# Making the first two tiles of W_out beside the last T stage, with their rows and turned halves in freed token spaces

## The chip, the cores and the metric

The kernel runs on one core of a Trainium2 chip. The metric is the device time of one execution in microseconds. A profiled execution gives a trace of every instruction on the core's engines: PE (TensorE matmul), PEld (its weight load), DVE (VectorE), ACT (ScalarE), POOL (GpSimd), and SP (SyncE), whose queue issues all the DMAs here. SP takes its DMAs strictly one after the other, and each waits for its own data and buffers.

## The reference

A two-layer encoder trunk on 2048 tokens of width 1024. Per layer, eight heads of banded softmax attention with a relative bias and four heads of chunkwise retention share one input projection, and their gated outputs go through `W_out` onto the residual:

```python
def hybrid_layer(x, norm_gain, w_in, w_out, rel_bias, cos, sin):
    hn = rms_norm(x, norm_gain)
    proj = hn @ w_in.astype(hn.dtype)
    aq, ak, av, ag, rq, rk, rv, rg = jnp.split(proj, cuts, axis=-1)
    ya = chunked_rel_attention(aq, ak, av, rel_bias)      # own chunk of 64 and 8 before it
    yr = chunkwise_retention(rq, rk, rv, cos, sin)        # with an RMS norm per head
    y = jnp.concatenate([ya * silu(ag), yr * silu(rg)], axis=-1)
    return x + y @ w_out

def reference(x, positions, norm_gain, w_in, w_out, rel_bias, final_gain):
    cos, sin = rotary_tables(positions, RET_HEAD_DIM)
    for layer in range(2):
        x = hybrid_layer(x, norm_gain[layer], w_in[layer], w_out[layer], rel_bias[layer], cos, sin)
    return rms_norm(x, final_gain)
```

## The kernel before

**Numbers.** Every large product is made in three float16 terms: each operand is split into an upper half and a rest ("hi" and "lo", "h" and "l"), and high·high, high·low and low·high are summed in PSUM. So each tile that a matmul uses exists as two float16 tiles.

**Stages.** A layer goes through four slices of heads (`s` = 0 to 3: two attention heads and one retention head each), and in each slice through four groups of 512 tokens (`n` = 0 to 3). For each `(s, n)` there are two dense stages: **T** (`dense_T`, L731), which makes q, k and the rotated retention q and k with features on partitions, and **V** (`dense_V`, L752), which makes the values and gates with tokens on partitions. Each stage has 96 matmuls in twelve parts ("thirds"). Attention and retention of the group before (`attention`, eight units of one 128-token tile and one head, three steps each) are interleaved: one step per third, so that its 24 steps lie beside one T and one V stage. After the last group of the last slice, **wout** (L1105) runs 16 token tiles × 6 rounds of 8 matmuls, and attention of the last group lies beside its first 24 rounds.

**Order.** The orders on PE, ACT, DVE and POOL are those in which the program records the instructions. SP's order is chosen by the scheduler, which moves loads to earlier places. Smaller work comes as generators that are pushed on a list (`push(gen, steps)`) and taken from its front (`pull`). `run` spreads the steps that the list still owes over the thirds that are left:

```python
for _ in gen:
    tick()
    if att[0] is not None and next(att[0], att) is att:
    ...
    if bg:
        pull(min(-(-todo // max(left, 1)), todo))
    left -= 1
```

`later(k, fn)` puts a function off by `k` thirds, and `tick` runs those that are due.

**An attention unit** (`qk`). PE makes S (L800, L801) in a PSUM tile of which there is one. DVE adds the bias and takes the maximum (L804, L806) into an `sc` buffer, ACT takes the exponential (L807) and its upper half into a `pq` buffer (L809), POOL makes the rest (L810). One third later a DMA transpose turns `pq` into `pT` (L812), and PE multiplies it with the values (L820 to L822) two units later. The tags `sc`, `pq` and `pT` have two buffers each.

**The output tiles.** Slices write their parts of a token tile's `y` to DRAM (`y_d`). For `wout` each tile comes back (`y_load`, L944), gets a power-of-two scale from its sum of squares (`y_squares` on ACT, L958; `y_scale`, five small DVE operations from L961), is split into two float16 rows (`rows_hi` on ACT, L227; `rows_lo` on DVE, L233), and both are turned by a DMA transpose (`y_turn`, L236 and L237). The rows come from `row_pair`, one buffer of tag `sc` and one of `pq`, that is from attention's two-buffer rings. The turned halves go into the tags `tabc` and `tabs` (even tiles) or `qq` and `swp` (odd tiles), which T stages use for the rotary tables and for q and k on their way (L670 is the multiplication with the tables). The residual's x is loaded into the space of a token group (`x_load`, L953).

**Token spaces.** `hT_of(l, n)` gives two float16 tiles (hTh, hTl) of 8 × 512 columns for the normalised tokens of group n. There are four such pairs. The spaces of one layer are handed to the next in the order of first request. After slice 3 has passed group n, its space is no longer read.

**Around the change.** `wout_first` makes the rows of tiles 0 and 1 and turns tile 0. It is pushed after the T stage of `(3, 3)`, with ten steps. `prep_O(l, 1)`, which converts the second half of `W_out` (L330 on ACT, L333 on DVE), is pushed right behind it with nine, so that both lie beside the V stage of `(3, 3)`. Tile 1 is turned in wout's second round (by program order). `rests` (L766 to L770) are the DVE operations that release a V stage's PSUM tile, one third after its matmuls.

Of the kernel before, what the change touches and what calls it, by code (L numbers as in the profile page):

```python
# [10 lines left out]
F32 = mybir.dt.float32  # L11
# [7 lines left out]
P = 128  # L19
# [8 lines left out]
def hybrid_trunk(ctx: ExitStack, tc: tile.TileContext, x, pos, gain, gcol, w_in, w_out, rel, fgain,  # L28
                 invf, dmask, dcol, out):
    nc = tc.nc  # L30
    SEQ, D = x.shape
    DEPTH = w_in.shape[0]
    KT = D // P
    NT = SEQ // P
    NS = SEQ // 512
    NSW = 4
# [119 lines left out]
    def gain_load(l):  # L156
        g = gains[l]
        g.b = cp.tile([P, D], F32, tag="gb", name=f"gb{l}")
        sp.dma_start(g.b, gain[l:l + 1, :].to_broadcast([P, D]))
# [40 lines left out]
    hT = {}  # L200
# [14 lines left out]
    def hT_of(l, n):  # L215
        if (l, n) not in hT:
            hT[l, n] = (hp.tile([P, KT, 512], F16, tag="hTh", name=f"hTh{l}_{n}"),
                        hp.tile([P, KT, 512], F16, tag="hTl", name=f"hTl{l}_{n}"))
        return hT[l, n]

    def row_pair(nm):
        return (b2.tile([P, 1280], F16, tag="sc", name=f"rh{nm}")[:, 0:D],
                b2.tile([P, 1280], F16, tag="pq", name=f"rl{nm}")[:, 0:D])

    def rows_hi(rows, xt, s_=None):

        act.activation(rows[0], xt, AF.Copy, scale=1.0 if s_ is None else s_[:, 0:1])  # L227

    def rows_lo(rows, xt, s_=None):
        if s_ is None:  # L230
            dve.tensor_tensor(rows[1], xt, rows[0], op=ALU.subtract)
        else:
            dve.scalar_tensor_tensor(out=rows[1], in0=xt, scalar=s_[:, 0:1], in1=rows[0], op0=ALU.mult, op1=ALU.subtract)  # L233

    def transpose_rows(rows, dh, dl):
        sp.dma_start_transpose(out=dh, in_=rows[0])  # L236
        sp.dma_start_transpose(out=dl, in_=rows[1])  # L237
# [350 lines left out]
    def flow(k=0):  # L588

        if len(pipe) > k:  # L590
            pipe.pop(0)()
# [344 lines left out]
    def y_load(l, t):  # L936
        u = St()
        u.nm = f"y{l}_{t}"
        u.t = t
        if t < 8:  # L940
            u.y = w4.tile([P, D], F32, tag="w4", name=f"yy{u.nm}")
        else:
            u.y = b2.tile([P, D], F32, tag="q", name=f"yy{u.nm}")
        sp.dma_start(u.y, y_d[t])  # L944
        return u

    def x_load(l, u):
        if l + 1 == DEPTH or u.t < 12:
            f = (hT[l, 0] if l + 1 == DEPTH else hT_of(l + 1, NS - 1))[u.t // 2 % 2].rearrange("p k c -> p (k c)").bitcast(F32)
            u.x = f[:, u.t % 2 * D:(u.t % 2 + 1) * D]  # L950
        else:
            u.x = w4.tile([P, D], F32, tag="w4", name=f"xx{u.nm}")
        sp.dma_start(u.x, x[u.t * P:(u.t + 1) * P, :] if l == 0 else x_d[u.t])  # L953

    def y_squares(u):
        u.m = b2.tile([P, 1], F32, tag="ym", name=f"ym{u.nm}")
        u.rows = row_pair(u.nm)
        act.activation(u.rows[0], u.y, AF.Square, accum_out=u.m)  # L958

    def y_scale(u, go):  # L960
        dve.tensor_scalar(u.m, u.m, 2.0 ** -100, None, op0=ALU.max)  # L961
        u.sy, iy = norm_scale(u.m, u.nm)
        u.sc = b2.tile([P, 1], F32, tag="osc", name=f"osc{u.nm}", bufs=4)
        dve.tensor_tensor(u.sc, iy, go.oi, op=ALU.mult)

    def y_turn(u):
        if u.t + 1 == NT:
            u.h, u.lo = (b2.tile([P, 10, P], F16, tag="pT", name=f"y{c}{u.nm}")[:, 0:KT, :] for c in "hl")
        else:
            u.h = b1.tile([P, KT, P], F16, tag=("tabc", "qq")[u.t % 2], name=f"yh{u.nm}")  # L970
            u.lo = b1.tile([P, KT, P], F16, tag=("tabs", "swp")[u.t % 2], name=f"yl{u.nm}")
        transpose_rows(u.rows, u.h, u.lo)
# [78 lines left out]
        sp.dma_start(out[t * P:(t + 1) * P, :], xt)  # L1051

    def wout_first(l, go, us):
        us.append(y_load(l, 0))
        x_load(l, us[0])
        us.append(y_load(l, 1))
        u, v = us
        for fns in ((), (lambda: y_squares(u),), (lambda: y_scale(u, go),), (lambda: rows_hi(u.rows, u.y, u.sy),),
                    (lambda: rows_lo(u.rows, u.y, u.sy), lambda: y_squares(v)), (lambda: y_turn(u), lambda: y_scale(v, go)),
                    (lambda: rows_hi(v.rows, v.y, v.sy),), (lambda: rows_lo(v.rows, v.y, v.sy),)):  # L1060
            yield
            for fn in fns:
                fn()
        yield

    def wout(l, go, gc, us, wT=None):

        end = l + 1 == DEPTH
        halves = [(t, c) for t in range(NT) for c in range(2)]
        if not end:  # L1070
            halves[-3], halves[-2] = halves[-2], halves[-3]
        events = {}
        for r in range(6 * NT):
            T, i = divmod(r, 6)
            t, c = halves[r // 3]
            u = us[t]
            if ring["att_done"] and i % 3 == 1:
                flow()
            for fn in events.pop(r, ()):
                fn()  # L1080
            hurry = T + 3 == NT and not end
            if i == 0 and 0 < T < NT - 1 and (end or T + 2 < NT):
                rows_lo(us[T + 1].rows, us[T + 1].y, us[T + 1].sy)
            if (i == 1 and T + 1 < NT and (end or T + 2 < NT)) or (i == 5 and hurry):
                y_turn(us[T + 1 if i == 1 else T + 2])
            if i == 0 and T + 2 < NT:
                us.append(y_load(l, T + 2))
            if i == 1 and T + 1 < NT:
                x_load(l, us[T + 1])
            if T + 2 < NT:  # L1090
                v = us[T + 2]
                if i == 3 - hurry:
                    y_squares(v)
                if i == 4 - hurry:
                    y_scale(v, go)
                if i == 5 - hurry:
                    rows_hi(v.rows, v.y, v.sy)
                    if hurry:
                        rows_lo(v.rows, v.y, v.sy)
            if i % 3 == 0:  # L1100
                ps = psD.tile([P, 512], F32, tag="dense", name=f"dO{l}_{t}_{c}")
            for m in range(8 * (i % 3), 8 * (i % 3) + 8):
                kt, w = divmod(m, 3)
                h_, w_ = ((u.h, gc[c].vh), (u.h, gc[c].vl), (u.lo, gc[c].vh))[w]
                pe.matmul(ps, h_[:, kt, :], w_[:, kt, :], start=(m == 0), stop=(m == 23))  # L1105
            if i % 3 == 2:
                xs = u.x[:, c * 512:(c + 1) * 512]
                keep(dve.scalar_tensor_tensor(out=xs, in0=ps, scalar=u.sc[:, 0:1], in1=xs, op0=ALU.mult, op1=ALU.add))
                if end and t + 1 == NT:
                    final_half(t, u.x, c)  # L1110
                if c == 1:
                    at = lambda k, fn, r=r: events.setdefault(r + k, []).append(fn)
                    if not end:
                        sp.dma_start(x_d[t], u.x)
                        rows = [w_[:, 2 + t % 2].rearrange("p k c -> p (k c)") for w_ in (wT.g.h, wT.g.l)]
                        residual(l + 1, t, u.x, at, rows if t < 4 else None, 4 < t < 12 and t % 4 > 0)
                    elif t + 1 < NT:
                        final(t, u.x, at)
            yield
        rest = [fn for r in sorted(events) for fn in events[r]]  # L1120
        push((fn() for fn in rest), len(rest))
        yield
# [5 lines left out]
    def push(gen, steps):  # L1128
        bg.append([gen, steps])
# [132 lines left out]
            self.s = [s_.bitcast(F32)[:, k:k + 1] for k in range(w)]  # L1262
            self.i = [i_.bitcast(F32)[:, k:k + 1] for k in range(w)]

    far = [hT_of(0, n) for n in (0, NS - 1, NS - 2)][1:]
    late = [h_.rearrange("p k c -> p (k c)").bitcast(F32)[:, i * D:(i + 1) * D] for f in far for h_ in f for i in range(2)]
    vst = [late[4 + j].rearrange("p (k c) -> p k c", c=P) for j in range(4)]
    x_in(0)
# [102 lines left out]
    for l in range(DEPTH):  # L1371
        gO = [Grp(), Grp()]
        go = Grp()
        for s in range(NSW):
            g = grp(l, s)
            for n in range(NS):
# [26 lines left out]
                        push(prep_O(l, 0, gO[0], go), 9)  # L1403
                if n == NS - 1 and s == 1 and l + 1 < DEPTH:
                    gain_load(l + 1)
                if not first:
                    run(dT, att, 10 if n == 0 else 14 if (l, s, n) == (0, 0, NS - 1) else 22 if (l, s) == (0, 0) else 24)
                if n == NS - 1 and s == NSW - 1:
                    us = []
                    push(wout_first(l, go, us), 10)  # L1410
                if n == 2 and s == 2:
                    push(prep_Omax(l, go), 13)
                if n == NS - 1:
# [19 lines left out]
        if l + 1 == DEPTH:  # L1433
            ring["fg"] = b3.tile([P, D], F32, tag="wh", name="fg")
            sp.dma_start(ring["fg"], fgain.to_broadcast([P, D]))
        wT = Sections(l + 1, 0, grp(l + 1, 0), True) if l + 1 < DEPTH else None
        wo = wout(l, go, gO, us, wT)

        def rounds_of(k):
# [76 lines left out]
```

## Time and profile before

| what | us |
|---|---|
| median of three timed runs | 2095.43 (2093.11 to 2095.86) |
| the profiled execution | 2094.75 |
| its span in the trace | 2092.8 |
| PE busy in the span | 2004.4 (96%) |
| DVE, ACT, POOL busy | 1343.8, 1141.3, 432.9 |
| mean granted TensorE clock | 0.991 |

In the trace, layer 0's T stage of `(3, 3)` runs from 833.4 to 859.4 us, its V stage to 893.2, and its wout stage to 1086.9. In layer 1 the same three run from 1846.3 to 1872.3, to 1906.0, and to 2085.5. A matmul's row has its start and its own length, which is longer than the distance to the next one since matmuls are pipelined. The pace is the distance between starts.

### The profile page before, as it was taken

What the parts mean: (1) busy time and instruction counts of PE and PEld (TensorE: products, weight loads), DVE (VectorE), ACT (ScalarE), POOL (GpSimd) and SP (SyncE); (2) the same over time, 40 slices, a digit from 0 to 9 for tenths busy, and PEclk for the clock granted to TensorE, in tenths of its full rate; (3) what the DMA queues carried; (4) which work ended last, traced back from release to release, by engine and by line L of the source; (5) the groups of instructions that cost most, each with busy time, mean ns of one, the idle gap of its engine ahead of it and who ended that gap; (6) DMA issues with size and microseconds to landing.
All of it is one profiled execution on the core that took longest, in us unless ns stands there. A gap on an engine that the chain in (4) does not pass through costs nothing.

```text
span 2092.8 us, 39599 instructions
## 1 busy us (share of the span) xinstructions
PE 2004.4 (96%) x14014; PEld 1049.4 (50%) x14014; DVE 1343.8 (64%) x4031; ACT 1141.3 (55%) x2522; POOL 432.9 (21%) x509
## 2 busy tenths in 40 slices
PE   6888999999999999998999999999999999998998
PEld 4344455555555555444444555555555555554443
DVE  7676666666656666576654666666666667656643
ACT  7455665556565654455444546554655565455432
POOL 1022222222122212121000222222222222222100
PEclk9999999999999999999999999999999999999999
DMA  8767674557476764599965556655655776558874
GB/s 247 171 127 162 136 166 114 115 112 159 110 169 133 161 166 99 113 211 260 219 185 113 120 102 142 130 121 106 155 123 118 178 156 162 117 100 183 212 199 123
DMA packets 645702, 313.65 MB, mean 150 GB/s; under 512 B 459232, under 2 KB 602080, under 8 KB 645504
## 3 DMA queue, kind: packets, MB, share of 16 engines
q1 hardware_dynamic: 645504, 311.12, 66.4%
q8 instruction: 110, 1.80, 0.4%
q14 instruction: 88, 0.72, 0.1%
HBM read 123.26 MB, written 41.98 MB: 79 GB/s over the span
## 4 chain that ended last, share of the span: by engine, by line
PE 55%; DMA 7%; DVE 5%; ACT 3%; issue 1%; SPq 1%; POOL 0%; POOLq 0%; DVEq 0%; ACTq 0%
PE dT L731 18%; PE dV L752 15%; PE dO L1105 12%; DMA pT<-pq 2%; PE r L860 2%; PE S L801 2%; PE S L800 2%; PE o L820 1%; PE o L821 1%; PE o L822 1%; DVE sc L804 1%; DMA swp<-rot 1%; DMA yhy<-rhy 1%; ACT sc L807 1%; ACT pq L809 1%
## 5 line engine op out<-in xcount | busy, mean ns | idle before, releaser
L810 POOL TENSOR_TENSOR pq<-sc,pq 128x640 f16<-128x640 f32 (+4 forms) x256 | 323.8, 1265 | 1175.9 <-issue 590.7
L807 ACT ACTIVATE sc<-sc,mq,cT 128x640 f32<-128x640 f32 (+4 forms) x256 | 218.5, 853 | 558.1 <-DVE mq L806 413.7
L752 PE MATMUL dV<-whV,hTh 128*128 128x512 f16 x1024 | 354.5, 382 | 13.0 <-DVE gt L770 12.8
L731 PE MATMUL dT<-hTh,whT 128*128 128x512 f16 x1008 | 349.4, 382 | 14.7 <-DMA hTh<-hTl 9.6
L752 PE MATMUL dV<-wlV,hTh 128*128 128x512 f16 x1024 | 354.1, 381 | 0.0
L752 PE MATMUL dV<-whV,hTl 128*128 128x512 f16 x1024 | 354.0, 381 | 0.0
L731 PE MATMUL dT<-hTl,whT 128*128 128x512 f16 x1008 | 346.6, 379 | 0.0
L731 PE MATMUL dT<-hTh,wlT 128*128 128x512 f16 x1008 | 346.6, 379 | 0.0
L752 PEld LDWEIGHTS <-hTh 128*128 128x128 f16 x2048 | 197.3, 98 | 227.7 <-DVE gt L770 16.4
L731 PEld LDWEIGHTS <-whT 128*128 128x128 f16 x2016 | 192.9, 98 | 221.6 <-issue 24.1
L804 DVE CUSTOM_DVE_ANT_0 sc<-S,bias 128x640 f32<-128x640 f32 (+4 forms) x256 | 188.4, 736 | 78.8 <-PE S L801 61.1
L1105 PE MATMUL dO<-whO,yly 128*128 128x512 f16 x512 | 194.1, 379 | 2.4 <-DMA yly<-rly 2.4
L1105 PE MATMUL dO<-whO,yhy 128*128 128x512 f16 x512 | 194.0, 379 | 1.2 <-DVE gt L770 0.6
L1105 PE MATMUL dO<-wlO,yhy 128*128 128x512 f16 x512 | 194.0, 379 | 0.0
L809 ACT ACTIVATE pq<-sc 128x640 f16<-128x640 f32 (+4 forms) x256 | 171.5, 670 | 10.9 <-DMA pT<-pq 3.0
L1105 PEld LDWEIGHTS <-yhy 128*128 128x128 f16 x1024 | 99.6, 98 | 115.1 <-issue 0.8
L752 PEld LDWEIGHTS <-hTl 128*128 128x128 f16 x1024 | 99.7, 98 | 105.0 <-issue 2.8
L800 PE MATMUL S<-k,q 128*128 128x128 f16 (+3 forms) x592 | 143.1, 268 | 7.9 <-DVE mq L804 7.9
L731 PEld LDWEIGHTS <-wlT 128*128 128x128 f16 x1008 | 97.2, 98 | 101.8 <-issue 1.1
L820 PE MATMUL o<-v,pT 128*128 128x65 f16 x1120 | 129.6, 193 | 10.2 <-DMA pT<-pq 9.7
L801 PE MATMUL S<-k,q 128*128 128x128 f16 (+3 forms) x592 | 130.5, 268 | 0.0
L820 PEld LDWEIGHTS <-pT 128*128 128x128 f16 x1120 | 105.3, 97 | 49.2 <-DMA pT<-pq 21.3
(350 smaller groups left out, 3352.7 us busy)
## 6 DMA issues: line engine op xcount, KB each, us to landing
q<-qq SPq DMA_DIRECT2D x128, 128.0 KB, 2.7
yyy<-y_d SPq DMA_DIRECT2D x32, 512.0 KB, 4.6
stT<-in_w_in_dram SPq DMA_DIRECT2D x27, 512.0 KB, 4.8
stV<-in_w_in_dram SPq DMA_DIRECT2D x26, 512.0 KB, 4.5
k<-kk SPq DMA_DIRECT2D x128, 64.0 KB, 2.0
swp<-rot SPq DMA_DIRECT2D x64, 128.0 KB, 2.5
tabc<-tab SPq DMA_DIRECT2D x32, 256.0 KB, 2.7
tabs<-tab SPq DMA_DIRECT2D x32, 256.0 KB, 2.9
```

Source lines behind the costliest of these rows:

```text
L731: pe.matmul(ps, w_[:, j, kt, :], h_[:, kt, :], start=(m == 0), stop=(m == 23))
L752: pe.matmul(ps, h_[:, kt, a * P:(a + 1) * P], w_[:, kt, :], start=(m == 0), stop=(m == 23))
L800: pe.matmul(o, st.q[:, hx, 0, cs], k_, start=True, stop=False)
L801: pe.matmul(o, st.q[:, hx, 1, cs], k_, start=False, stop=True)
L804: dve.tensor_tensor_reduce(out=v, in0=S[:, 0:w], in1=g.bias[hx][:, 640 - w:640], scale=1.0, scalar=-3.0e38, op0=ALU.add, op1=ALU.max, accu ...
L807: act.activation(v, v, AF.Exp, bias=m[:, 0:1], scale=g.c[:, 0:1])
L809: act.activation(pq[:, 0:w], v, AF.Copy)
L810: pool.tensor_tensor(pq[:, w:2 * w], v, pq[:, 0:w], op=ALU.subtract)
L820: pe.matmul(o[:, 0:65], u.p[:, b, :], v_[:, 0:65], start=(b == 0), stop=False)
L821: pe.matmul(o[:, 0:64], u.p[:, b, :], v_[:, 65:129], start=False, stop=False)
L860: pe.matmul(out_, w_, m_, start=(i == 0), stop=(i + 1 == len(pairs)))
L1105: pe.matmul(ps, h_[:, kt, :], w_[:, kt, :], start=(m == 0), stop=(m == 23))
```

## The change

- `wout_first` is pushed before the T stage of `(3, 3)`, with 14 steps, and now makes both tiles wholly, with their transposes. By the changed program's order its first twelve steps (tile 0 whole, tile 1 up to its squares) lie beside T, and the rest of tile 1 beside the start of V.
- `areas(l)` names three freed token spaces: those that the next layer's groups 3, 1 and 2 will use (in the last layer the spaces of its own groups 0, 1 and 2). The first holds x, as before.
- The rows of tiles 0 to 5 (in the last layer of all tiles) lie in quarters of the second and third space instead of the `sc` and `pq` rings. The turned halves of tiles 0 and 1 lie in the second space instead of `tabc`, `tabs`, `qq` and `swp`.
- `wout` no longer turns tile 1.
- The first request for the layer-0 spaces is in the order 0, 1, 2, 3 (it was 0, 3, 2, 1).
- On SP, as the scheduler orders it, tile 0's transposes stand before the attention transpose of the third unit of `(3, 2)`, and tile 1's before that of the sixth. In layer 0 the x loads of tiles 2 and 3 stand at the start of wout, where they stood in slice 3's first groups.

PE's instructions keep their number and order.

```diff
+    def areas(l):
+
+        if l + 1 == DEPTH:
+            return [hT[l, i] for i in range(3)]
+        return [hT_of(l + 1, i) for i in (NS - 1, 1, 2)]
+
+    def quarter(area, i):
+        return area[i // 4].rearrange("p k c -> p (k c)")[:, i % 4 * D:(i % 4 + 1) * D]
+
     def x_load(l, u):
         if l + 1 == DEPTH or u.t < 12:
-            f = (hT[l, 0] if l + 1 == DEPTH else hT_of(l + 1, NS - 1))[u.t // 2 % 2].rearrange("p k c -> p (k c)").bitcast(F32)
+            f = areas(l)[0][u.t // 2 % 2].rearrange("p k c -> p (k c)").bitcast(F32)
...
-    def y_squares(u):
+    def y_squares(l, u):
         u.m = b2.tile([P, 1], F32, tag="ym", name=f"ym{u.nm}")
-        u.rows = row_pair(u.nm)
+        if u.t < 6 or l + 1 == DEPTH:
+            i = (u.t + 2) % 6 * 2
+            u.rows = [quarter(areas(l)[2 - i // 8], (i + j) % 8 if i < 8 else 4 + (i + j) % 4) for j in range(2)]
+        else:
+            u.rows = row_pair(u.nm)
         act.activation(u.rows[0], u.y, AF.Square, accum_out=u.m)
...
-    def y_turn(u):
-        if u.t + 1 == NT:
+    def y_turn(l, u):
+        if u.t < 2:
+            u.h, u.lo = (quarter(areas(l)[1], 2 * u.t + i).rearrange("p (k c) -> p k c", c=P) for i in range(2))
+        elif u.t + 1 == NT:
...
     def wout_first(l, go, us):
+        areas(l)
         us.append(y_load(l, 0))
         x_load(l, us[0])
         us.append(y_load(l, 1))
-        u, v = us
-        for fns in ((), (lambda: y_squares(u),), (lambda: y_scale(u, go),), (lambda: rows_hi(u.rows, u.y, u.sy),),
-                    (lambda: rows_lo(u.rows, u.y, u.sy), lambda: y_squares(v)), (lambda: y_turn(u), lambda: y_scale(v, go)),
-                    (lambda: rows_hi(v.rows, v.y, v.sy),), (lambda: rows_lo(v.rows, v.y, v.sy),)):
-            yield
-            for fn in fns:
-                fn()
-        yield
+        for r in range(6):
+            u = us[r // 3]
+            if r % 3 == 0:
+                yield
+                yield
+                y_squares(l, u)
+                yield
+                yield
+                y_scale(u, go)
+            elif r % 3 == 1:
+                rows_hi(u.rows, u.y, u.sy)
+                yield
+                rows_lo(u.rows, u.y, u.sy)
+            else:
+                y_turn(l, u)
+            yield
...
-            if (i == 1 and T + 1 < NT and (end or T + 2 < NT)) or (i == 5 and hurry):
-                y_turn(us[T + 1 if i == 1 else T + 2])
+            if (i == 1 and 0 < T < NT - 1 and (end or T + 2 < NT)) or (i == 5 and hurry):
+                y_turn(l, us[T + 1 if i == 1 else T + 2])
...
-    far = [hT_of(0, n) for n in (0, NS - 1, NS - 2)][1:]
+    far = [hT_of(0, n) for n in range(NS)][:1:-1]
...
+                if n == NS - 1 and s == NSW - 1:
+                    us = []
+                    push(wout_first(l, go, us), 14)
                 if not first:
                     run(dT, att, 10 if n == 0 else 14 if (l, s, n) == (0, 0, NS - 1) else 22 if (l, s) == (0, 0) else 24)
-                if n == NS - 1 and s == NSW - 1:
-                    us = []
-                    push(wout_first(l, go, us), 10)
```

More of the change, by code (lines that the diff above doesn't have):

```diff
@@ L1092, in wout @@
                 if i == 3 - hurry:
-                    y_squares(v)
+                    y_squares(l, v)
                 if i == 4 - hurry:
```

## The prediction

> **What bounds the kernel now.** First I read the page's head: the span and TensorE's line.
>
> ```profile
> span 2092.8 us, 39599 instructions
> PE 2004.4 (96%) x14014; PEld 1049.4 (50%) x14014; DVE 1343.8 (64%) x4031; ACT 1141.3 (55%) x2522; POOL 432.9 (21%) x509
> ```
>
> TensorE (PE) is busy for 2004.4 of 2092.8 us, so the kernel is bound by matmuls that this change leaves in number and in order (the two programs' PE orders differ only in tile names). A gain can come only from stretches in which PE stands still or runs slowly. So the next view is busy time by stretch. The rows are, in this order: the V stage of s = 2, group 3 (layer 0); the V stage of s = 3, group 2; then T and V of s = 3, group 3 in layer 0, and the same two in layer 1. Columns: start:end and length, then busy time with instruction counts of PE, PEld, DVE, ACT, POOL, then the granted clock, the DMA share and GB/s.
>
> ```profile
> 653.90:680.20 26.30, 26.30 (x212) 14.59 (x210) 21.20 (x65) 17.36 (x41) 6.95 (x8) 1.00 0.54 114
> 807.20:833.40 26.20, 26.20 (x210) 14.50 (x208) 19.46 (x57) 14.19 (x36) 6.87 (x8) 1.00 0.44 94
> 833.40:859.40 26.00, 26.00 (x203) 13.95 (x201) 13.76 (x38) 11.24 (x25) 6.61 (x7) 1.00 0.54 110
> 859.40:893.20 33.80, 29.62 (x209) 15.39 (x206) 20.98 (x62) 18.83 (x40) 5.65 (x7) 0.90 0.69 125
> 1846.30:1872.30 26.00, 26.00 (x202) 13.96 (x200) 13.61 (x38) 11.23 (x26) 6.62 (x7) 1.00 0.61 110
> 1872.30:1906.00 33.70, 28.41 (x210) 15.12 (x206) 20.97 (x62) 18.81 (x40) 5.62 (x7) 0.95 0.64 136
> ```
>
> A V stage has the same matmuls each time and needs 26.2 to 26.3 us. The last one of each layer, the one that carries `wout_first`, takes 33.8 and 33.7, with PE idle in part and a granted clock of 0.90 and 0.95. It is not the load on DVE or ACT: 21.20 and 17.36 us of them fit into 26.30 without a PE gap. The waits of that V stage (who waited for whom, total, times, longest), and then the timelines of DVE and SP (start, length, idle time before in brackets), say what it is.
>
> ```profile
> DVE sc L804 <- DMA yhy<-rhy: 5.1, 1, 5.1
> PE S L800 <- DVE mq L804: 3.3, 1, 3.3
> ```
> ```profile
> 871.49 0.68 DVE L670 TENSOR_TENSOR raw<-raw,tabc 128x512 f32<-128x512 f32 x1
> 877.29 0.82 DVE L804 CUSTOM_DVE_ANT_0 sc<-S,bias 128x640 f32<-128x640 f32 x1 [5.11 <-DMA yhy<-rhy]
> ```
> ```profile
> 872.45 2.08 SPq L236 DMA_TRANSPOSE yhy<-rhy  x1
> ```
>
> The rows of tile 0 sit in one of the two `sc` buffers. Attention's next L804 needs that buffer and is stuck behind the transpose that reads it. The transpose could not start either, because it writes `tabc`, which L670 reads until 872.2. It was issued at 872.45, and DVE stood until 877.29. No score left PSUM, so PE stopped too. PE's timeline, both layers:
>
> ```profile
> 878.17 0.27 PE L800 MATMUL S<-k,q 128*128 128x128 f16 x1 [3.28 <-DVE mq L804]
> 879.19 0.63 PE L752 MATMUL dV<-wlV,hTh 128*128 128x512 f16 x1
> 879.62 0.63 PE L752 MATMUL dV<-whV,hTh 128*128 128x512 f16 x1
> 885.75 0.39 PE L752 MATMUL dV<-whV,hTh 128*128 128x512 f16 x1 [0.64 <-DVE gt L770]
> 885.98 0.38 PE L752 MATMUL dV<-whV,hTl 128*128 128x512 f16 x1
> 1891.00 0.27 PE L800 MATMUL S<-k,q 128*128 128x128 f16 x1 [3.18 <-DVE mq L804]
> 1892.02 0.63 PE L752 MATMUL dV<-wlV,hTh 128*128 128x512 f16 x1
> 1898.59 0.39 PE L752 MATMUL dV<-whV,hTh 128*128 128x512 f16 x1 [1.88 <-DVE gt L770]
> ```
>
> After the 3.28 us gap the matmuls follow each other every 0.43 us (879.19 to 879.62). Further on it is 0.23 (885.75 to 885.98). So the gap costs itself and a stretch at half speed behind it.
>
> **The change part by part.**
>
> *The V stages.* All of `wout_first`'s buffers move: the rows to free quarters of the spaces of token groups 1 and 2, the turned halves of tiles 0 and 1 to group 1's. `sc`, `pq`, `tabc` and `qq` serve their own users again, so L804 and the transpose have nothing to wait for. The price of the stall is the excess over the heaviest clean V stage: 33.80 − 26.30 = 7.5 in layer 0 and 33.70 − 26.30 = 7.4 in layer 1, together **14.9 us**. What comes next is the clean stage's pace, 26.3. [...]
>
> *The work moved into T.* Durations (minimum, median, maximum in ns, first and last start):
>
> ```profile
> L958 ACT ACTIVATE rhy<-yyy x32: 1039/1041/1057, 866.4 to 2056.3; 128x1024 f16<-128x1024 f32 x32
> L227 ACT ACTIVATE rhy<-yyy,sy x32: 1132/1143/1149, 868.5 to 2062.1; 128x1024 f16<-128x1024 f32 x32
> L233 DVE SCALAR_TENSOR_TENSOR rly<-yyy,sy,rhy x32: 1270/1277/1340, 870.0 to 2065.5; 128x1024 f16<-128x1024 f32 x32
> L961 DVE TENSOR_SCALAR ymy<-ymy x32: 143/147/155, 867.6 to 2061.5; 128x1 f32<-128x1 f32 x32
> ```
>
> In the changed program's order, T receives both squares and one `rows_hi` on ACT (2 × 1.04 + 1.14 = 3.2) and, on DVE, one `rows_lo` and ten one-column operations (1.28 + 10 × 0.15 = 2.8). T goes from 11.24 to 14.4 on ACT and from 13.76 to 16.6 on DVE; V falls to 15.6 and 18.2. All four lie under the 17.36 and 21.20 that a clean stage of this length carries, so I cost them at nothing. Their cover is PE's 26 us of matmuls. If it failed, the price would be one operation's length at a time, some 1.3 us.
>
> *The DMAs moved with it.* SP is one queue in order. In the changed order tile 0's two transposes and one `w_out` load stand before the attention transpose of group 2's third unit, and tile 1's two, a load and two `y_d` stores before that of the sixth. Rows: in layer 0 the end of the third unit's maximum on DVE, SP before it, the unit's issue and PE's use of it; then a `w_out` load, the issue lengths of row transposes, the landing of attention's, and one that landed in a crowd.
>
> ```profile
> 850.26 0.21 DVE L806 TENSOR_SCALAR mq<-mq,ncT 128x1 f32<-128x1 f32 x1
> 851.42 0.59 SPq L652 DMA_DIRECT2D k<-kk  x1
> 853.81 1.32 SPq L812 DMA_TRANSPOSE pT<-pq  x1
> 861.23 0.19 PE L820 MATMUL o<-v,pT 128*128 128x65 f16 x1
> 871.34 0.39 SPq L294 DMA_DIRECT2D stO<-in_w_out_dram  x1
> L236 SPq DMA_TRANSPOSE yhy<-rhy x32: 1232/1238/2446, 872.5 to 2063.3; - x32
> DMA to landing us min/median/max: 2.3/3.4/6.0
> 891.42 2.56 SPq L812 DMA_TRANSPOSE pT<-pq  x1
> 897.15 0.20 PE L820 MATMUL o<-v,pT 128*128 128x65 f16 x1 [1.46 <-DMA pT<-pq]
> ```
>
> The unit has 861.23 − 853.81 = 7.4 us, of which the landing takes 3.4 (the median for L812): 4.0 to spare. `rows_lo` of tile 0 stands right behind that L806 on DVE, so its rows are there at 850.5 + 1.3 = 851.8, and SP is done with `k` at 852.0. Two issues of 1.24 and a load of 0.39 end at 854.9, so the attention transpose goes out 1.1 late. In a crowd its landing grows to 897.15 − 891.42 = 5.7, or 2.3 more. 1.1 + 2.3 is under 4.0, so a bare fit. If both issues took the maximum 2.45 it would be 3.5 + 2.3 − 4.0 = 1.8 over. The bounds per tile are 0 and 1.8, four tiles in all: 0 to 7.2. I take 0.7 in all, near the lower end, because the median issue is the rule and the maximum the exception.
>
> *The start of the W_out stage.* Behind the slow V stage PE meets late things:
>
> ```profile
> 893.80 0.38 PE L1105 MATMUL dO<-whO,yhy 128*128 128x512 f16 x1 [0.62 <-DVE gt L770]
> 1906.64 0.38 PE L1105 MATMUL dO<-whO,yhy 128*128 128x512 f16 x1 [0.62 <-DMA yyy<-y_d]
> 1909.05 0.20 PE L820 MATMUL o<-v,pT 128*128 128x65 f16 x1 [0.53 <-DMA pT<-pq]
> 938.66 0.20 PE L820 MATMUL o<-v,pT 128*128 128x65 f16 x1 [1.88 <-DMA pT<-pq]
> 953.88 0.20 PE L820 MATMUL o<-v,pT 128*128 128x65 f16 x1 [2.19 <-DMA pT<-pq]
> ```
>
> The transposes of tile 1 and three loads were packed around 891.42, and the gap of 1.46 is theirs; 0.53 is the same in layer 1. With an orderly V stage these go, and so do the two gaps of 0.62: bounds 0 and 1.46 + 0.53 + 0.62 + 0.62 = 3.2. I take 2.8, since two loads of x move in exchange from early s = 3 to the start of layer 0's W_out, where they meet the first attention transposes (half of what 2 × 0.4 of issue would cost, an estimate). The gaps of 1.88 and 2.19 come later, when the residual's transposes share SP with attention's. The change leaves those in place, so I keep them: bounds 0 and 4.1 of gain, taken as 0.
>
> *Nothing else.* In layer 1 all later rows leave `sc` and `pq` too, but attention is over by then.
>
> **The sum.** 14.9 − 0.7 + 2.8 = 17.0 us. The profiled execution took 2094.75 (span 2092.8 and 1.95 around it), 0.68 under the median of the three timed runs, 2095.43. On the profiled one it gives 2077.75, on the median **2078.4**.
>
> **The rivals.**
>
> *A. The moved transposes crowd attention's.* All four tiles pay the 1.8 above, and at the start of W_out the 1.46 stays too, so that 0.62 + 0.62 + 0.53 = 1.8 comes: 14.9 − 7.2 + 1.8 = 9.5, so 2085.9. For it: the spare is 4.0 and the crowd is real. Against it: the T stages show no PE gap at all.
>
> *B. Only the one long stall goes.* The `rests` on DVE stay late (gaps of 0.64 and 1.88 behind L770), because `prep_O` still crowds the V stage. Then about 2.5 of the 14.9 stays: 14.5, so 2080.9. Against it: a V stage with 21.20 on DVE has no such gap.
>
> *C. The slow clock is not the gap's.* [...] It is at most what the gaps leave of the excess: 7.5 − 3.28 − 0.64 = 3.6 and 7.4 − 3.18 − 1.88 = 2.3, together 5.9: 17.0 − 5.9 = 11.1, so 2084.3. Against it: no slow matmul in the rows stands anywhere but behind such a gap. [...]
>
> *D. Slower.* SP stands on a turned tile whose rows are late, as it stood at 872.45, but now in T, with attention's transposes behind it. `pq` is then not freed, ACT and DVE stop, and PE with them. If that cost a full V-stage stall of 7.5 at each of the four tiles, it would be 4 × 7.5 − 14.9 − 2.8 = 12.3 slower, 2107.7. It turns slower than before from 4.4 us a tile (17.7 / 4). For that the transpose must go out 4.0 + 4.4 = 8.4 us late, while two issues at the maximum and a load make 3.5. So unlikely.
>
> *E. It does not do what it says*: a reader of the token spaces ends later than I think, and `y_squares` waits in T. Group 2's last reader is the V stage that ends at 833.40, before T. Then about no change.
>
> **How the numbers follow.** Forecast 0.66, A 0.12, B 0.08, C 0.04, E 0.03, D 0.07. The range goes down to no new cost and both later gaps gone (14.9 + 3.2 + 4.1 = 22.2, so 2073.2) and up to A (2085.9); B and C lie inside. A measurement of this kernel can tell 0.2% (4.2 us) from no change: faster 0.90, same 0.03, slower 0.07.
>
> **What would show it.** Right: last V stages of 26 to 27 us with clock 1.00, no L804 wait for a row transpose, T stages still at 26.0, attention transposes of the third and sixth unit issued 1 to 2 us later against their use with no PE gap. Wrong: PE gaps at L820 in T (A, or D if DVE's L804 waits too), gaps behind L770 (B), half-speed matmuls without a gap (C). A V stage still over 30 us would fell the whole argument.

## The result and the profile after

The changed kernel takes 2081.61 us (median of four runs, 2080.88 to 2085.9) against 2095.34 for the kernel before (four runs). The ratio is 0.9943 with a 95% interval of 0.993 to 0.9956, so it is faster by 13.7 us: only 0.6%, but the interval lies clear of 1. The profiled execution took 2085.9 us, the slowest of the four. It reaches T of (3, 3) in layer 0 3.2 us later than the profiled execution before did, with the same matmuls up to there. Among the experiments below the same distance runs from 3.1 us later (e2) to 2.8 us earlier (e5), and e3, which is the changed program up to there, comes 0.3 us earlier than before. So it is not the change's, and I compare stage by stage and not by the span.

The page's head after: PE's busy time is unchanged but for 0.9 us.

```profile
span 2084.1 us, 39559 instructions
PE 2005.3 (96%) x14014; PEld 1051.2 (50%) x14014; DVE 1345.9 (65%) x4031; ACT 1141.0 (55%) x2522; POOL 435.8 (21%) x509
```

Busy time by stretch (columns as in the prediction): T and V of (3, 3) in layer 0, the same two in layer 1, and a part of layer 0's W_out stage.

```profile
836.65:862.70 26.05, 26.05 (x203) 13.99 (x201) 14.66 (x43) 13.92 (x28) 6.66 (x7) 1.00 0.67 133
862.70:890.50 27.80, 26.70 (x208) 14.32 (x206) 20.20 (x58) 16.24 (x37) 5.88 (x7) 1.00 0.67 144
1842.90:1869.00 26.10, 26.10 (x204) 14.00 (x202) 14.66 (x43) 13.96 (x29) 6.71 (x7) 1.00 0.72 137
1869.00:1897.40 28.40, 26.88 (x208) 14.37 (x206) 20.20 (x58) 16.24 (x37) 5.85 (x7) 1.00 0.61 128
926.00:970.00 44.00, 40.13 (x257) 19.40 (x253) 29.19 (x78) 23.24 (x44) 11.29 (x11) 0.96 1.11 252
```

T is as it was. The V stages are at full clock, but not at the 26.1 us of a V stage without a gap. These two stretches end where W_out's first matmul starts, and so hold a gap of 0.62 that the windows of before left out. From first matmul to first matmul, V went from 34.30 to 27.79 in layer 0 and from 34.21 to 28.39 in layer 1. The waits of the two V stages (layer 0, then layer 1) say what is left:

```profile
DVE rot L670 <- DMA swp<-rot: 5.4, 1, 5.4
...
PE dV L752 <- DVE gt L770: 0.4, 1, 0.4
```
```profile
DVE rot L670 <- DMA swp<-rot: 6.0, 1, 6.0
...
PE dV L752 <- DVE gt L770: 0.8, 1, 0.8
```

The wait of DVE's score addition (L804) for a row transpose is gone. In its place DVE stands 5.4 and 6.0 us at the rotary multiplication L670, for a transfer that swaps the halves of the rotated q or k (`swp`) and reads what L670 writes over. It is one row, here before and after in layer 0:

```profile
858.60 1.92 DVE L670 TENSOR_TENSOR rot<-rot,tabc 128x512 f32<-128x512 f32 x1 [1.94 <-DMA y_d<-yr]
865.26 0.69 DVE L670 TENSOR_TENSOR rot<-rot,tabc 128x512 f32<-128x512 f32 x1 [5.38 <-DMA swp<-rot]
```

Before, DVE already stood there 1.94 us. It waited for the swap and for the store issued right behind it, and the profile names the one that landed last. SP's queue shows why the swap is late. First the transfer's first row before, then SP after:

```profile
855.35 0.52 SPq L666 DMA_DIRECT2D swp<-rot  x1
```
```profile
855.13 1.26 SPq L236 DMA_TRANSPOSE hTh<-hTl  x1
856.48 1.29 SPq L237 DMA_TRANSPOSE hTh<-hTl  x1
857.83 0.58 SPq L294 DMA_DIRECT2D stO<-in_w_out_dram  x1
858.51 2.80 SPq L812 DMA_TRANSPOSE pT<-pq  x1
861.49 0.47 SPq L666 DMA_DIRECT2D swp<-rot  x1
```

Against the start of its V stage the swap went out 4.15 us early before (855.35 against 859.50) and only 1.2 us early after (861.49 against 862.72). Ahead of it stand tile 0's two transposes, a load of `W_out`, and an attention transpose that took 2.80 us to issue where it took 1.32 before. DVE runs late from there on, `rests` with it, and PE meets it (idle time in brackets):

```profile
890.51 0.38 PE L1129 MATMUL dO<-whO,hTh 128*128 128x512 f16 x1 [0.62 <-DVE gt L770]
...
897.58 0.38 PE L1129 MATMUL dO<-wlO,hTh 128*128 128x512 f16 x1 [0.51 <-DVE wlO L333]
...
934.96 0.20 PE L820 MATMUL o<-v,pT 128*128 128x65 f16 x1 [2.06 <-DMA pT<-pq]
...
936.43 0.63 PE L1129 MATMUL dO<-whO,yly 128*128 128x512 f16 x1
936.86 0.63 PE L1129 MATMUL dO<-whO,yhy 128*128 128x512 f16 x1
```

The W_out stages kept their lengths: 192.96 to 192.90 in layer 0 and 178.85 to 179.38 in layer 1 (there to the end of the last matmul).

### The profile page after: what moved, and what is told of

It reads as the page before. It is cut to its first block, busy times and chain, and to the rows that moved or that the text cites. A ratio compares the mean times of both kernels' runs of the same rounds, so it can differ in the third digit from the quotient of the medians.

```text
span 2084.1 us, 39559 instructions
## 1 busy us (share of the span) xinstructions
PE 2005.3 (96%) x14014; PEld 1051.2 (50%) x14014; DVE 1345.9 (65%) x4031; ACT 1141.0 (55%) x2522; POOL 435.8 (21%) x509
## 5 line engine op out<-in xcount | busy, mean ns | idle before, releaser
L752 PEld LDWEIGHTS <-hTh 128*128 128x128 f16 x2048 | 196.6, 98 | 223.1 <-DVE gt L770 13.7
L804 DVE CUSTOM_DVE_ANT_0 sc<-S,bias 128x640 f32<-128x640 f32 (+4 forms) x256 | 188.6, 737 | 70.5 <-PE S L801 64.5
L1129 PE MATMUL dO<-whO,yly 128*128 128x512 f16 x448 | 170.3, 380 | 2.2 <-DMA yly<-rly 1.5
L1129 PE MATMUL dO<-whO,yhy 128*128 128x512 f16 x448 | 170.3, 380 | 0.4 <-DMA yhy<-hTh 0.4
L1129 PE MATMUL dO<-wlO,yhy 128*128 128x512 f16 x448 | 170.2, 380 | 0.0
L1129 PEld LDWEIGHTS <-yhy 128*128 128x128 f16 x896 | 87.5, 98 | 101.9 <-issue 1.1
L820 PE MATMUL o<-v,pT 128*128 128x65 f16 x1120 | 130.4, 194 | 8.1 <-DMA pT<-pq 7.6
L821 PE MATMUL o<-v,pT 128*128 128x64 f16 x1120 | 130.6, 195 | 0.0
```

The lines of the kernel that those rows point to most:

```text
L752: pe.matmul(ps, h_[:, kt, a * P:(a + 1) * P], w_[:, kt, :], start=(m == 0), stop=(m == 23))
L804: dve.tensor_tensor_reduce(out=v, in0=S[:, 0:w], in1=g.bias[hx][:, 640 - w:640], scale=1.0, scalar=-3.0e38, op0=ALU.add, op1=ALU.max, accu ...
L820: pe.matmul(o[:, 0:65], u.p[:, b, :], v_[:, 0:65], start=(b == 0), stop=False)
L821: pe.matmul(o[:, 0:64], u.p[:, b, :], v_[:, 65:129], start=False, stop=False)
```

## The experiments

Three questions were put. Does the gain come from the new spaces or from the new time? Which of the two spaces held the stall? And is SP's order what is left? All ratios are against the kernel before on the same chip (its median was 2094.85 in the runs of e1 to e5 and 2094.46 in those of e6 to e9, eleven runs each). Stage lengths are from first matmul to first matmul, as above.

### The new spaces at the old time (e1_space_only)

Rows and halves as in the change, but `wout_first` with its old steps behind T, and tile 1 turned in W_out's second round:

```diff
-        for r in range(6):
-            u = us[r // 3]
...
+        u, v = us
+        for fns in ((), (lambda: y_squares(l, u),), (lambda: y_scale(u, go),), (lambda: rows_hi(u.rows, u.y, u.sy),),
...
-            if (i == 1 and 0 < T < NT - 1 and (end or T + 2 < NT)) or (i == 5 and hurry):
+            if (i == 1 and T + 1 < NT and (end or T + 2 < NT)) or (i == 5 and hurry):
...
-                if n == NS - 1 and s == NSW - 1:
-                    us = []
-                    push(wout_first(l, go, us), 14)
                 if not first:
...
+                if n == NS - 1 and s == NSW - 1:
+                    us = []
+                    push(wout_first(l, go, us), 10)
```

> Only the spaces are new: rows and turned halves lie in the freed token spaces, but the first two tiles are made where they were, beside the last V stage (ten steps after T), and tile 1 is turned in the W_out stage. Theory 1 (the long V stage came from attention's buffers being lent to the rows and from the turned half waiting for the table buffer): the 5.1 us wait of L804 for a row transpose is gone, the V stage falls from 33.8 to 27 to 29 us in both layers, time 2081 to 2086 us. Theory 2 (it came from nineteen steps of small work crowded into twelve thirds): the V stage stays above 31, time above 2090.

Measured: 2082.72 us (2080.49 to 2087.99), ratio 0.9944 [0.993, 0.9959], with V stages of 27.74 and 27.75. So the new spaces alone give what the whole change gives. What this V stage still shows among its waits is DVE standing for the squares on ACT, which lie in V here. Whether that wait is what keeps V above 26.09 was not tested by itself:

```profile
DVE ymy L974 <- ACT hTl L971: 3.1, 1, 3.1
```

### The new time with the rows in the ring (e2_time_only)

The change, but all rows come from `row_pair` again. The halves of tiles 0 and 1 stay in the freed space.

```diff
-        if u.t < 6 or l + 1 == DEPTH:
+        if False:
```

> Only the time is new: the first two tiles are made beside T as in the change, but all rows come from attention's rings again (the turned halves of tiles 0 and 1 must lie in the freed space, since T uses the table buffers). Theory 1: the same stall appears again, now in T and at the start of V: L804 of the third unit waits until tile 0's row transpose has landed, behind the k transfers on SP, 5 to 6 us; T goes from 26.1 to 29 to 33, the time is 2088 to 2104 us. Theory 2: most of the gain stays, T 26 to 27, V 27 to 28, time 2080 to 2084.

Measured: 2076.96 us (2074.65 to 2081.06), ratio 0.9916 [0.9902, 0.993]. This is below the range of either theory. T is at 26.08 and both V stages are clean:

```profile
862.59:888.68 26.09, 26.09 (x208) 14.40 (x206) 21.10 (x59) 16.16 (x37) 5.80 (x7) 1.00 0.77 155
1868.16:1894.25 26.09, 26.09 (x207) 14.38 (x205) 21.10 (x59) 16.18 (x37) 5.81 (x7) 1.00 0.68 148
```

A cost of rows in the ring did not come: in T no L804 wait for a transpose shows. This kernel is even ahead of the change, but it differs from it in a second thing. The scheduler put the load of `W_out` behind the swap, which went out 3.8 us before the V stage instead of 1.2.

### Tile 0's transposes behind the swap (e3_turn_behind_swap)

The change with one move on SP: tile 0's two transposes are recorded two thirds later and kept in program order, which puts them behind the `swp` transfers. The load of `W_out` stays ahead of them.

```diff
+            if pin:
+                tc.keep_in_program_order(i)
...
+            elif r == 2:
+                later(2, lambda u=u: y_turn(l, u, True))
             else:
                 y_turn(l, u)
```

> The change with one thing moved: tile 0's two transposes are pinned on SP behind the two transfers that swap q's halves (swp from rot), instead of before them. Theory 3 (what is left of the long V stage comes from those transfers standing behind the turned tile: DVE's L670 waits 5.4 us for them): the wait falls to under 3 us, V goes from 27.8 and 28.4 to 26.2 to 27.2, time 2077 to 2080.5. Rival (the rest is the load of prep_O late in V): V stays at 27.5 to 28.5, time 2081 to 2083.

Measured: 2076.17 us (2075.13 to 2076.87), ratio 0.9908 [0.9896, 0.9921]. The interval lies wholly below the change's, and the median a little below the expected range. T is at 26.08, both V stages at 26.09, and W_out at 191.22 and 178.08:

```profile
859.20:885.29 26.09, 26.09 (x207) 14.42 (x205) 21.05 (x59) 16.23 (x37) 5.85 (x7) 1.00 0.73 153
```

So what was left of the stall is the swap's place on SP. The load of `W_out` also moved here: in layer 0 it goes out 2.9 us earlier against V's start than in the change. A late load is not the cause instead, for in e2 it goes out 2.9 us later than in the change, and V is clean.

### Both tiles one stage earlier (e5_beside_v_of_group_2)

`wout_first` is pushed ahead of the V stage of (3, 2), so that most of its work lies beside that stage. The rows of tiles 0 and 1 lie in the second of the three spaces, with three pauses fewer between the steps.

```diff
-                if n == NS - 1 and s == NSW - 1:
-                    us = []
-                    push(wout_first(l, go, us), 14)
...
+                if n == NS - 2 and s == NSW - 1:
+                    us = []
+                    push(wout_first(l, go, us), 12)
```

> The first two tiles are made one stage earlier, beside V of slice 3, group 2 (13 steps with two idle ones taken out, rows of tiles 0 and 1 in the space of group 1, of tiles 2 to 5 in that of group 2), so that the last T stage carries nothing and the last V stage only prep_O. Theory 3: no wait of L670 for swp over 2.5 us in the last V stage, which takes 26.1 to 26.8; V of group 2 stays at 26.1 to 26.6; time 2076 to 2079.5. Rival (prep_O's load): last V stage 27.5 or more, time 2080.5 to 2083; a third way is that V of group 2 pays for it, 27 or more.

Measured: 2077.7 us (2073.91 to 2080.2), ratio 0.9914 [0.99, 0.9929]. The V stage of (3, 2), T and V of (3, 3) are all at 26.08 to 26.09, the pace without a gap:

```profile
804.54:830.63 26.09, 26.09 (x208) 14.39 (x206) 21.23 (x66) 16.06 (x38) 6.80 (x7) 1.00 0.75 172
830.63:856.71 26.08, 26.08 (x204) 14.03 (x202) 14.80 (x40) 12.94 (x29) 7.62 (x7) 1.00 0.81 152
856.71:882.80 26.09, 26.09 (x208) 14.43 (x205) 22.02 (x54) 15.85 (x35) 5.85 (x7) 1.00 0.63 138
```

Another place serves as well: in layer 0's T and V of (3, 3) no wait of DVE for the swap over 0.6 us shows. It cannot be told from e2 or e3 by time.

### Only the halves moved (e6_halves_only)

The kernel before, with the halves of tiles 0 and 1 in the freed space (here and in e7 the spaces are requested in the change's order):

```diff
-        if u.t + 1 == NT:
+        if u.t < 2:
+            u.h, u.lo = (quarter(areas(l)[1], 2 * u.t + i).rearrange("p (k c) -> p k c", c=P) for i in range(2))
+        elif u.t + 1 == NT:
```

> The kernel before with one thing changed: the turned halves of tiles 0 and 1 lie in the freed space, while the rows stay in attention's sc and pq buffers and all steps keep their old time and order. Theory H (the stall came from the halves' buffers: the transpose waited for tabc and so held the sc buffer): the last V stages fall from 34.3 to 27 to 29 us and the total to 2081 to 2086. Theory R (the stall came from rows in attention's ring beside V, whatever the halves do, because SP comes to the transpose at 872.4 anyway): the last V stages stay at 32 to 34 us with DVE's score addition waiting 4 to 5 us for a row transpose, total 2090 to 2095. If both buffers count, something between, about 2088.

### Only the rows moved (e7_rows_only)

The kernel before, with the rows in the freed spaces:

```diff
-        u.rows = row_pair(u.nm)
+        if u.t < 6 or l + 1 == DEPTH:
+            i = (u.t + 2) % 6 * 2
+            u.rows = [quarter(areas(l)[2 - i // 8], (i + j) % 8 if i < 8 else 4 + (i + j) % 4) for j in range(2)]
+        else:
+            u.rows = row_pair(u.nm)
```

> The kernel before with the other thing changed: the rows lie in the freed spaces, while the turned halves stay in tabc, tabs, qq and swp and all steps keep their old time and order. Theory H: SP still stands before the transpose until the rotary multiplication has left tabc at 872.2, so the attention transposes behind it are late: last V stages 30 to 34 us, total 2088 to 2095. Theory R: attention's score buffers are free, the transposes hold nobody, the last V stages fall to 27 to 28 us and the total to 2081 to 2085, as with both spaces moved.

Measured: 2084.25 us for the halves (2082.17 to 2087.0, ratio 0.9948 [0.9934, 0.9962]) and 2086.08 for the rows (2079.81 to 2090.08, 0.9954 [0.9937, 0.9971]). V is 28.57 twice with the halves moved, 27.74 and 27.75 with the rows moved. Each theory expected its own run to gain and the other not to, and both runs gained about what the whole change does (the rows' median lies 1.1 us above the range given for it). SP and DVE with the halves moved, then with the rows moved:

```profile
867.29 1.23 SPq L236 DMA_TRANSPOSE hTh<-rhy  x1
```
```profile
870.49 0.82 DVE L804 CUSTOM_DVE_ANT_0 sc<-S,bias 128x640 f32<-128x640 f32 x1 [0.74 <-DMA hTh<-rhy]
```
```profile
870.37 1.94 SPq L236 DMA_TRANSPOSE yhy<-hTl  x1
```
```profile
869.98 0.82 DVE L804 CUSTOM_DVE_ANT_0 sc<-S,bias 128x640 f32<-128x640 f32 x1
```

With the rows moved the transpose still waits for `tabc`. It goes out 12.96 us into the V stage (V starts at 857.41), as before (872.45 against 859.50 is 12.95). But nobody needs its source, and L804 runs without a wait. With the halves moved the transpose goes out 10.2 us into the stage, 2.7 earlier, and L804 waits 0.74 instead of 5.11. The stall needed both links: an attention buffer held by a transpose, and that transpose held by `tabc`. Neither run brings V to 26.09. Gaps behind L770 stay (1.13 and 0.62 us with the halves moved, 0.30 and 0.62 with the rows moved, in layer 0).

### The load off SP (e8_load_on_scalar_queue)

The change with the load of `W_out` that stood ahead of the swap issued by ScalarE, at its place in the V stage:

```diff
-            sp.dma_start(st, v)
+            (eng or sp).dma_start(st, v)
...
+                sts.append(load_sec(w_out[l, :, o:o + P], f"{nm}{j + 1}", eng=act if (c, j) == (1, 0) else None))
```

> The change as it is, except that one load of W_out (the second block of its second half), which stood on SP between tile 0's transposes and attention's, is issued by ScalarE in the V stage. Theory 'sum on SP' (turn, load and the lengthened attention transpose together make the rotary swap 2.9 us late, and either one taken away is enough): last V stages 26.1 to 26.6, DVE's wait for the swap 2 to 4 us, total 2076 to 2078. Rival 'the turn alone' (two row transposes right ahead lengthen the attention transpose's issue to 2.8 us, the load is not needed for it): last V stages still 27.5 to 28.4 and the wait 5 to 6 us, total 2081 to 2082.

Measured: 2079.51 us (2076.56 to 2082.27), ratio 0.992 [0.9906, 0.9935], between the two expectations. The attention transpose's issue fell from 2.80 to 1.38 and the wait at L670 from 5.4 and 6.0 to 2.7 and 2.3. V is 26.36 in layer 0 and 27.26 in layer 1. For the swap the sum on SP is thus confirmed: without the load, tile 0's two transposes alone do not make it late enough for DVE to stand longer than in e3. Most of the missing rest of layer 1 is a wait of PE for an attention transpose; why that one landed late is not shown:

```profile
DVE rot L670 <- DMA swp<-rot: 2.7, 1, 2.7
```
```profile
1890.01 0.20 PE L820 MATMUL o<-v,pT 128*128 128x65 f16 x1 [0.99 <-DMA pT<-pq]
```

### New time, halves moved, transposes behind the swap (e9_time_halves_turn_behind)

e3 and e2 together: rows in the ring, tile 0's transposes behind the swap. Its edits are those two.

> The change with the rows of all tiles back in attention's sc and pq buffers and with tile 0's two transposes behind the rotary swap on SP. If rows in the ring cost nothing beside T, and the swap's place in the queue is the rest, the last V stages are 26.1 and the total 2075 to 2077.5, the best of the versions or level with the best. If the rows' space is what makes the early turn safe, attention's score additions wait for the later transposes: V stages 27 to 30, total 2079 to 2086.

Measured: 2075.89 us (2074.56 to 2077.57), ratio 0.9908 [0.9894, 0.9921], level with e3 and the lowest median. Both T and V stages are clean, and SP shows the swap in its old place:

```profile
856.73:882.82 26.09, 26.09 (x208) 14.42 (x205) 21.11 (x59) 17.20 (x37) 6.28 (x7) 1.00 0.73 151
1861.18:1887.27 26.09, 26.09 (x208) 14.42 (x205) 21.10 (x59) 17.19 (x37) 6.24 (x7) 1.00 0.73 144
```
```profile
851.15 1.25 SPq L814 DMA_TRANSPOSE pT<-pq  x1
852.62 0.57 SPq L668 DMA_DIRECT2D swp<-rot  x1
853.25 0.59 SPq L669 DMA_DIRECT2D swp<-rot  x1
853.88 0.58 SPq L929 DMA_DIRECT2D y_d<-yr  x1
854.51 1.24 SPq L237 DMA_TRANSPOSE hTh<-rhy  x1
```

Up to tile 0's transposes SP's order is that of e3, and the two programs differ in the rows alone. So the rows' move out of the ring is not needed once the work lies beside T. Laid side by side, with the swap's issue counted back from the start of layer 0's V stage and DVE's wait in that layer:

| kernel | swap issued before V (us) | DVE's wait for it | V, layer 0 and 1 |
|---|---|---|---|
| the change | 1.2 | 5.4 | 27.79, 28.39 |
| e8, load off SP | 3.3 | 2.7 | 26.36, 27.26 |
| e2, rows in the ring | 3.8 | 2.2 | 26.09, 26.09 |
| e3, transposes behind | 3.9 | 2.8 | 26.09, 26.09 |
| e9, e2 and e3 | 4.1 | 2.7 | 26.09, 26.09 |

## Why the prediction was right, and where it was off

**The stall.** Right in cause, and shown from both sides by e6 and e7. The prediction named both buffers; what it did not say is that freeing either one takes nearly all of it.

**Its size.** Predicted 14.9, with V falling to 26.3. From first matmul to first matmul the V stages gained 34.30 − 27.79 = 6.5 and 34.21 − 28.39 = 5.8, together 12.3; the gap of 0.62 stands ahead of W_out before and after. Without it they are 27.17 and 27.77, outside the 26 to 27 that was named as the sign. The missing 2.6 are in the next step but one.

**Work moved into T at no cost.** Right. T stays at 26.08 by its matmuls in both layers. DVE carries 14.66 there, less than the 16.6 that I counted, and 20.20 in V where I counted 18.2, so some 2 us of it still lie in V. I had counted ten one-column operations into T, but T receives the five of tile 0 (tile 1's come at 869.06, in V), and the late L670 slid from T into V.

**The moved DMAs.** This is the step that failed. For the transfer that it weighed it was nearly exact: in layer 0 the third unit's transpose went out 1.48 late (1.1 predicted), landed in 5.34 (5.7) and left 0.60 before PE used it, with no gap. The sixth unit's went out 18.3 us into its V stage, where e3 has it at 16.1, and landed just as PE needed it (PE stood 0.14 us). But I counted that transpose as if it were the only one behind the moved transposes. Behind it stand the two `swp` transfers, and DVE waits for those; it did so before the change, so they had little to spare. I did not follow SP one row further. The price was not 0.7. Taken from e3, whose one edit is that order, it is 27.79 − 26.09 = 1.7 and 28.39 − 26.09 = 2.3 in the V stages (the two gaps of 0.62 are in these). The W_out stages differ by another 1.68 and 1.30, which makes 7.0 in all by the profiled stages, and 5.4 by the medians (2081.61 − 2076.17, from different sets of runs). Not all of the 1.68 is the order's: about 1.3 is the half speed behind the 2.06 us gap (six matmuls at 0.43 instead of 0.21), and the longer gap that e3 has there brought none.

**The start of W_out.** Predicted 2.8, and nothing came. The 1.46 and the 0.53 went, but two gaps of 0.51 behind a late L333 came, both 0.62 stayed, and the later 1.88 and 2.19 turned into 2.06 and 0.61 with 3.4 us at half speed behind the first. In layer 1 a gap of 1.08 came (PE at L820, 1958.74). The stages changed by −0.06 and +0.53. In e3 no gap of over 0.3 is left at the start of W_out, in either layer, so the mechanism was right, and in the change the late DVE took the gain away.

**The sum.** By stages 6.51 + 5.83 + 0.06 − 0.53 = 11.9 against 17.0; by the medians 13.7. The 1.8 between the two lies within the spread of the changed kernel's four runs, 5.0. Both the V stages and the start of W_out fell short, so no two errors cancelled; the range was wide enough for them because it reached up to A. In e3 the same four stages give 8.21 + 8.13 + 1.74 + 0.77 = 18.9, and its median is 2.2 below the predicted 2078.4. The forecast was thus about the change with SP's order mended.

**The rivals.** B gave 2080.9 and is nearest to the measured 2081.61: only the long stall went, the `rests` stayed late, behind L770, and 2.6 of the 14.9 stayed (B said 2.5). Its cause was another, though. It blamed `prep_O`, which stands in the same V stage in e3, where no gap is left. A falls as priced, since T has no gap; its crowd on SP was real, but the swap paid for it and not attention. D falls too: SP issued tile 0's first transpose 0.09 us after it was done with `k`. E falls with the stall. C would have left slow matmuls in the V stages; in the rows above they are at clock 1.00.

## What to carry to other kernels

When a step is moved ahead on a DMA queue that goes in order, as SP's rows do here, go down the queue and give each transfer behind it its consumer and its slack, until one has more slack than the delay. Here the first had 4.0 us and passed. The second had little: DVE already waited 1.94 us for it, a wait of 2.8 (e3) still cost PE nothing, and 5.4 did. And the stall here, which ran through two held buffers, was broken at either one (V went from 34.30 and 34.21 to 28.57 twice in e6 and to 27.74 and 27.75 in e7), so the cheaper is worth trying alone.

## What the runs showed of the hardware

In these runs the length of a PE gap did not by itself decide whether half speed followed. After the 2.06 us gap in the change, dense matmuls followed each other every 0.43 us (936.43 to 936.86 above), and it took until 938.95 for full speed to come back (the next two are 0.22 apart). From 935 to 939 us the granted clock was 0.57. In e3 a longer gap had none behind it (PE's timeline of e3; the next dense matmuls are 0.21 apart, and from 922 to 966 us the granted clock was 1.00):

```profile
930.01 0.20 PE L822 MATMUL o<-v,pT 128*128 128x65 f16 x1 [2.65 <-DMA pT<-pq]
...
931.03 0.38 PE L1133 MATMUL dO<-whO,yly 128*128 128x512 f16 x1
931.24 0.38 PE L1133 MATMUL dO<-whO,yhy 128*128 128x512 f16 x1
```

In e6 a gap of the same length did (the pace is 0.43):

```profile
890.19 0.20 PE L820 MATMUL o<-v,pT 128*128 128x65 f16 x1 [2.65 <-DMA pT<-pq]
...
891.69 0.63 PE L1121 MATMUL dO<-wlO,hTh 128*128 128x512 f16 x1
892.12 1.06 PE L1121 MATMUL dO<-whO,hTh 128*128 128x512 f16 x2
```

Two shorter gaps say the same: one of 1.95 us in e7 had half speed behind it (L1121 at 890.30 and 890.73, 0.43 apart), and one of 2.51 in e2 had none (L1129 at 934.04 and 934.25, 0.21 apart; the granted clock was 1.00 from 925 to 968 us). What tells the gaps with half speed behind them from those without, no trace here shows.
